# Carrying a written-out instruction order from the up projection into the first six weight groups of a Winograd-form down projection, and moving two kinds of low parts to other units

## The chip, the cores and the metric

The kernel runs on one core of a Trainium2 chip. The metric is the device time of one execution in microseconds (us). Before the change three runs gave 781.72, 781.77 and 783.16 us; the median is 781.77 us.

## The reference, cut to what matters

One decoder layer on 512 tokens of width 1024: an mLSTM and a convolution group with one output projection, then a feed-forward block with a causal convolution of width 3. The change lies wholly in the second half of this feed-forward block:

```python
u = rms_norm(x, ffn_pre_g[l]) * (1.0 + sc2) + sh2
up = causal_dwconv(u @ ffn_up[l], ffn_conv_w[l], ffn_conv_b[l])   # 512 x 5632
a, gt = jnp.split(up, 2, axis=-1)
f = (jax.nn.silu(gt) * a) @ ffn_down[l]                            # 512 x 2816 by 2816 x 1024
x = x + g2 * rms_norm(f, ffn_post_g[l])
```

## The kernel before, in words

Every matrix product is taken in three matmuls (`mm3`, lines 188 to 190): each operand is split into a high part, rounded to the PE's fp32r type, and a low part, the rest. High times high, low times high and high times low are added in PSUM. The high part is a ScalarE copy; the low part is a subtraction, source minus high part. Three helpers make such pairs. `split` (lines 1013 and 1014) subtracts on VectorE. `w_split` (lines 170 and 171) subtracts on GpSimd. `added_split` (lines 1077 to 1079) has ScalarE write the negative of the high part as well and lets a transfer, issued on GpSimd's queue, add the source to it:

```python
S.activation(hi, src, AF.Copy)
S.activation(lo, src, AF.Copy, scale=-1.0)
G.dma_start(lo, src, accum_op=ALU.add)
```

The up projection makes 22 units, numbered 0 to 21, of 128 hidden features; a unit has a value half and a gate half. Units 8, 10, ... 20 are made in a Strassen-Winograd form: seven block products P1 to P7 over halves of the tokens and of the width, four of them opened by `first_products`, then the sums of `between` (lines 1102 to 1107), then the last three. Their odd neighbours are plain. The low part of the form S4, called p3, is made by `added_split`. After its products a unit goes through `conv3` (one ScalarE operation on line 995 and two VectorE operations on line 997 for each half), a silu (line 1132) and the product of value and gate (line 1133), which gives a half of F. Two units make one F, which is `a11, a21, a12, a22` in four quarters. `form_sums` (lines 1021 to 1024) and `form_parts` (lines 1029 to 1033) turn an F into the operands of the down projection: two pairs of high and low tiles (`fh`, `fl`), and two stores, on ScalarE's queue, of what the second stage needs (`g2d`).

The down projection takes the eleven Fs as eleven groups of weights, in the order 4, 5, ... 10, 0, 1, 2, 3 (`ORDER`); the weight groups are numbered by that order, so weight group 6 meets F10, and weight groups 7 to 10 meet F0 to F3, whose operands were written to DRAM and are fetched again by `reload` (line 1318, four transfers each on GpSimd's queue). The first stage makes P1, P5, P7 and P6 for every group, 24 matmuls each. For each group `load1` (lines 1173 and 1177) loads three quarters of 256 KB, `forms1` (lines 1183 to 1185, VectorE) makes three sums of them in place, and `parts1` splits the four forms b1, t1, t3, t2 and stores t2 for later (line 1190). The quarter b1 is not touched by the sums. The second stage makes P2, P3 and P4 with `load2`, `forms2` and `forms_g2`, 18 matmuls a group.

The buffers set much of the order. Weight parts lie in a ring of 20 tiles, two and a half groups. Raw weights lie in four buffers: two of the pool `raws`, which are the ones that held the up projection's raw weights, and two in `more`, which takes the place of `u2h`, the up projection's other operand, and so is free only when the last up-projection matmul has run. `wd_raw` chooses: groups with `m % 4 < 2` go to `raws`, the others to `more`; the first three groups have places of their own. The eight PSUM banks pass from the up projection to the down projection's accumulators: P1 takes two banks, P5 and P7 four, and P6 takes the two banks in which unit 21 lay, so P6 can't start before `conv3` has read unit 21, gate half last (`fg21c`).

What sets the order: PE's matmuls and SyncE's queue go as the code is written. VectorE, ScalarE and GpSimd are ordered by a scheduler, except inside a `with in_order():` block, where what the block holds keeps its written order on each engine. Such a block covers the up projection from unit 8 on and ends with F10's parts. Everything of the down projection after weight group 1 stands outside it:

```python
for m in range(SPILLED):
    reload(m)
for m in range(NM):
    if m > 1:
        forms1(m)
        parts1(m)
    if m + 3 < NM:
        load1(m + 3)
    else:
        load2(m + 3 - NM)
    if m < 5:
        load_g2(m)
    ...
    if m < M1:
        for which in ("p1", "p5", "p7", "p6"):
            prod1(m, which)
```

## Time and profile before

| what | value |
|---|---|
| median of the three runs | 781.77 us |
| the profiled execution: its own time, its span | 782.49 us, 780.8 us |
| PE busy | 757.5 us, 97% of the span |
| VectorE busy | 642.8 us, 82% |
| ScalarE busy | 451.2 us, 58% |
| GpSimd busy | 367.3 us, 47% |
| transfers | 149.00 MB, mean 191 GB/s |

The span runs from the first to the last instruction. The profiled execution's own time is 1.69 us over its span and 0.72 us over the median. Times in rows count from the start of the span. In a timeline the first number is the start, the second the duration, and what stands in square brackets is how long the engine had been idle and what it was waiting for. DVE is VectorE, ACT ScalarE, POOL GpSimd, SP SyncE; an engine's name with a q is its queue.

### The profile page before, as it was taken

To read this page: it belongs to the slowest core of one execution; us is meant where nothing else is said; L and a number is where in the kernel's file an instruction comes from. 1 tells how busy PE (TensorE), PEld (TensorE's weight loads), DVE (VectorE), ACT (ScalarE), POOL (GpSimd) and SP (SyncE) were. 2 spreads that over 40 slices of the span, in tenths; PEclk is the share of its full clock that TensorE was granted. 3 is DMA by queue.
4 is the path that set the end of the run, shared out by engine and by line. 5 is a ranking of instruction groups with operands and counts; after the bars stand their busy time and mean duration, and the time that the engine had idled before them with its cause. 6 is when DMAs were issued, how large, how long until landed. Compare 5 with 4: busy or idle time off the path is not lost.

```text
span 780.8 us, 11567 instructions
## 1 busy us (share of the span) xinstructions
PE 757.5 (97%) x3961; PEld 647.1 (83%) x3961; DVE 642.8 (82%) x1039; ACT 451.2 (58%) x862; POOL 367.3 (47%) x331
## 2 busy tenths in 40 slices
PE   7999999999999999999999999999999998699996
PEld 6888898778888788888889988899988897588885
DVE  6978999999999856837958499788889767898995
ACT  5557275777675266752435466667667674355762
POOL 1039487796796643452831355455455554000001
PEclk9999999999999999999999999999999999799999
DMA  8973225123031551528763598799997989588772
GB/s 330 393 278 121 83 61 186 50 82 108 28 136 54 189 189 55 176 95 288 279 216 135 162 221 238 207 255 240 242 248 185 225 214 317 171 318 253 242 256 107
DMA packets 55263, 149.00 MB, mean 191 GB/s; under 512 B 6402, under 2 KB 7842, under 8 KB 51108
## 3 DMA queue, kind: packets, MB, share of 16 engines
q1 hardware_dynamic: 31284, 96.18, 35.7%
q0 software_dynamic: 9632, 19.40, 12.5%
q10 hardware_dynamic: 14288, 32.68, 12.1%
q8 instruction: 31, 0.51, 0.3%
q14 instruction: 28, 0.23, 0.1%
HBM read 117.42 MB, written 15.61 MB: 170 GB/s over the span
## 4 chain that ended last, share of the span: by engine, by line
PE 58%; DVE 28%; DMA 5%; ACT 4%; issue 3%; POOL 1%; ACTq 0%; SPq 0%; DVEq 0%; POOLq 0%
DVE cv L731 10%; PE up L189 5%; PE up L190 4%; PE up L188 4%; PE p L1415 4%; PE glu L189 3%; PE glu L188 3%; PE glu L190 3%; PE p L189 2%; PE p L188 2%; PE p L190 2%; PE glu L316 2%; PE mixa L190 2%; PE mixa L188 2%; PE mixa L189 2%
## 5 line engine op out<-in xcount | busy, mean ns | idle before, releaser
L731 DVE SCALAR_TENSOR_TENSOR cv<-gt,cvw,cv 128x505 f32<-128x505 f32 (+24 forms) x200 | 137.4, 729 | 2.3 <-ACT cv L719 1.1
L685 POOL TENSOR_TENSOR ro2r<-ro2t,mhalf 128x1 f32<-128x1 f32 x1 | 0.6, 562 | 93.0 <-DVE ro2t L683 93.0
L727 POOL TENSOR_TENSOR cs<-cs,cs 128x510 f32<-128x510 f32 (+3 forms) x32 | 41.7, 1304 | 0.3
L725 ACT ACTIVATE cs<-gt,cvw 128x511 f32<-128x511 f32 (+4 forms) x40 | 27.4, 716 | 5.9 <-POOL cs L727 2.7
L189 PE MATMUL up<-u2l,wup_0h 128*128 128x512 f32 (+1 forms) x72 | 25.7, 356 | 0.2 <-DVE u2l L910 0.2
L188 PE MATMUL up<-u2h,wup_0h 128*128 128x512 f32 (+1 forms) x72 | 25.6, 356 | 0.0
L190 PE MATMUL up<-u2h,wup_0l 128*128 128x512 f32 (+1 forms) x72 | 25.5, 354 | 0.0
L171 POOL TENSOR_TENSOR wglu_0l<-wglu,wglu_0h 128x512 fp32r<-128x512 f32 x4 | 5.3, 1328 | 40.2 <-ACT wglu_0h L170 40.2
L171 POOL TENSOR_TENSOR wqko_1024l<-wqko,wqko_1024h 128x512 fp32r<-128x512 f32 x12 | 15.6, 1297 | 18.4 <-ACT wqko_1024h L170 12.9
L155 DVE SCALAR_TENSOR_TENSOR junk<-spare,cb 128x1024 bf16<-128x1024 f32 x12 | 19.0, 1584 | 3.3 <-DMA spare<-in_adaT 3.1
L155 DVE SCALAR_TENSOR_TENSOR junk<-ada,cb 128x1024 bf16<-128x1024 f32 x12 | 19.5, 1621 | 2.6 <-DMA ada<-in_adaT 2.4
L188 PE MATMUL qko<-uh,wqko_1024h 128*128 128x512 f32 x48 | 20.6, 430 | 0.0
L188 PE MATMUL qko<-uh,wqko_0h 128*128 128x512 f32 x48 | 20.2, 420 | 0.0
L276 DVE SCALAR_TENSOR_TENSOR junk<-ada,cb 128x1024 bf16<-128x1024 f32 x16 | 19.5, 1218 | 0.1
L171 POOL TENSOR_TENSOR wo_512l<-wo,wo_512h 128x512 fp32r<-128x512 f32 x8 | 12.9, 1615 | 13.6 <-ACT wo_512h L170 13.6
L171 POOL TENSOR_TENSOR wqko_0l<-wqko,wqko_0h 128x512 fp32r<-128x512 f32 x12 | 16.6, 1383 | 4.9 <-ACT wqko_0h L170 4.9
L190 PE MATMUL qko<-uh,wqko_1024l 128*128 128x512 f32 x48 | 18.8, 392 | 0.0
L190 PE MATMUL qko<-uh,wqko_0l 128*128 128x512 f32 x48 | 18.8, 391 | 0.0
L171 POOL TENSOR_TENSOR wqko_512l<-wqko,wqko_512h 128x512 fp32r<-128x512 f32 x12 | 17.0, 1420 | 3.7 <-ACT wqko_512h L170 3.7
L189 PE MATMUL qko<-ul,wqko_1024h 128*128 128x512 f32 x48 | 18.7, 390 | 0.0
L189 PE MATMUL qko<-ul,wqko_0h 128*128 128x512 f32 x48 | 18.7, 390 | 0.0
L190 PE MATMUL qko<-uh,wqko_512l 128*128 128x512 f32 x48 | 18.7, 389 | 0.0
(1233 smaller groups left out, 3128.8 us busy)
## 6 DMA issues: line engine op xcount, KB each, us to landing
wups<-in_w_up SPq DMA_DIRECT2D x56, 256.0 KB, 5.5
wqko<-in_w_qko SPq DMA_DIRECT2D x12, 1024.0 KB, 4.8
ada<-in_adaT ACTq DMA_DIRECT2D x20, 512.0 KB, 4.8
ada<-in_adaT SPq DMA_DIRECT2D x16, 512.0 KB, 6.7
wo<-in_w_out SPq DMA_DIRECT2D x8, 1024.0 KB, 4.8
wup<-in_w_up SPq DMA_DIRECT2D x8, 1024.0 KB, 6.2
spare<-in_adaT ACTq DMA_DIRECT2D x12, 512.0 KB, 7.2
wd<-in_w_down SPq DMA_DIRECT2D x20, 256.0 KB, 5.3
```

Of the source, the lines that this page charges most:

```text
L155: t = V.scalar_tensor_tensor(out=junk, in0=r, scalar=1.0, in1=cb, op0=ALU.mult, op1=ALU.mult, accum_out=mod[:, i : i + 1])
L171: (eng or G).tensor_tensor(out=lo[:, :n], in0=src, in1=hi[:, :n].bitcast(F32), op=ALU.subtract)
L188: PE.matmul(ps, a[0], b[0], start=start, stop=False)
L189: PE.matmul(ps, a[0], b[1], start=False, stop=False)
L190: PE.matmul(ps, a[1], b[0], start=False, stop=stop)
L276: V.scalar_tensor_tensor(out=junk, in0=first[k][:, i * D : (i + 1) * D], scalar=1.0, in1=cb, op0=ALU.mult, op1=ALU.mult, accum_out=part[k] ...
L316: PE.matmul(banks0[i], blk(wk, i)[a], u[k][b], start=k == 0 and a == b, stop=False)
L685: G.tensor_tensor(out=r, in0=t, in1=mhalf[:, :1], op=ALU.pow)
L725: S.activation(t[:, d:], cvx[j][:, : T - d], AF.Copy, scale=w(CK - 1 - d))
L727: G.tensor_tensor(out=side[:, d:], in0=side[:, d:], in1=t[:, d:], op=ALU.add)
L731: last_tap[0] = V.scalar_tensor_tensor(out=cp[:, d:], in0=cvx[j][:, : T - d], scalar=w(CK - 1 - d), in1=cp[:, d:], op0=ALU.mult, op1=ALU.add)
L1415: PE.matmul(ps[q], x, y, start=False, stop=m == NM - 1 and i == 2, skip_group_check=True)
```

## The change

What it does, part by part:

- **p3 of the up projection.** The low part of S4 is made by `w_split`, a subtraction on GpSimd, where a second ScalarE copy and an adding transfer made it.
- **b1 of the down projection.** For weight groups 0 to 5 the untouched quarter's low part is made by `added_split`, through the new `part_b`, where VectorE subtracted. Groups 6 to 10 stay as they were.
- **The order.** The block `in_order` now goes on through weight groups 0 to 5, with forms, parts, loads and products written out. `form_parts` is cut in two, `form_highs` and `form_lows`; for F9 the lows are made in weight group 3, and F10's sums and parts come in weight group 4. `between` of unit 20 comes ahead of `forms1(0)`.
- **PE.** P6 of weight group 0 comes after P1 and P5 of weight group 1.
- **Buffers.** `wd_raw` counts `(m - 3) % 4`, so groups 3 and 4 go to `raws` and groups 5 and 6 to `more`.
- **Transfers.** Loads of weight groups 3 and 4 are issued ahead of the last up-projection stores. The sixteen reload transfers, which stood first after the up projection on GpSimd's queue, come one F each in weight groups 5, 6, 7 and 8; the `g2` loads move from groups 0 to 4 to groups 5 to 9.

The core of the diff:

```diff
-    def form_parts(m, F):
+    def form_highs(m, F):
...
+    def form_lows(m, F):
         for (hi, lo), z in zip(pairs[m], (F[:, :T], ysum)):
             V.tensor_tensor(out=lo, in0=z, in1=hi.bitcast(F32), op=ALU.subtract)
...
     def wd_raw(m, n):
-        return raws.tile([P, 2048], F32, tag="raw", name=f"wd{n}_{m}") if m % 4 < 2 else more[:, m % 2, :]
+        return raws.tile([P, 2048], F32, tag="raw", name=f"wd{n}_{m}") if (m - 3) % 4 < 2 else more[:, m % 2, :]
...
+    def part_b(m):
+        w1[m] = {"b1": added_split(loaded[m][1], f"b1_{m}")}
+
+    def parts1(m, a=0, b=3):
+        r = loaded.pop(m) if b == 3 else loaded[m]
+        names = [] if m in w1 else [(f"b1_{m}", 1)]
+        names += [(f"t1_{m}", 2), (f"t3_{m}", 0), (f"t2_{m}", 3)][a:b]
+        w1[m] = w1.get(m, {}) | parts(r, names)
+        if b == 3:
+            nc.sync.dma_start(t2_d[m], r[3])
...
+    def opening_products(m):
+        for which in ("p1", "p5", "p7", "p6"):
+            if m == 1 and which == "p7":
+                prod1(0, "p6")
+            if m or which != "p6":
+                prod1(m, which)
...
-            weight_form(i, "p3", s4, added_split)
+            weight_form(i, "p3", s4)
...
+            between(i, *banks)
             if not more_to_come:
                 forms1(0)
-            between(i, *banks)
...
             else:
+                part_b(0)
+            va = conv3(pa, j, f"fa{j}")
+            if not more_to_come:
                 parts1(0)
                 forms1(1)
-            va = conv3(pa, j, f"fa{j}")
+                part_b(1)
+                for n in (3, 4):
+                    load1(n)
...
-        unit_out(bj, ba, conv3(bg, NF + bj, f"fg{bj}"), Fs[NM - 1])
-        form_sums(NM - 1, Fs[NM - 1])
-        form_parts(NM - 1, Fs[NM - 1])
+        load1(5)
+        bg = conv3(bg, NF + bj, f"fg{bj}")
...
+        opening_products(0)
+        part_b(2)
+        parts1(1, 2)
+        opening_products(1)
+        forms1(2)
+        unit_out(bj, ba, bg, Fs[NM - 1])
+        parts1(2)
+        opening_products(2)
+        for m in range(3, 6):
+            forms1(m)
+            part_b(m)
+            parts1(m)
+            load1(m + 3)
+            if m == 3:
+                form_lows(NM - 2, Fs[NM - 2])
+            elif m == 4:
+                form_sums(NM - 1, Fs[NM - 1])
+                form_parts(NM - 1, Fs[NM - 1])
+            if m > 4:
+                reload(m - 5)
+                load_g2(m - 5)
+            for which in ("p1", "p5", "p7", "p6"):
+                prod1(m, which)
...
-    for m in range(SPILLED):
-        reload(m)
-    for m in range(NM):
-        if m > 1:
-            forms1(m)
-            parts1(m)
+    for m in range(6, NM):
+        forms1(m)
+        parts1(m)
+        if m - 5 < SPILLED:
+            reload(m - 5)
```

**VectorE, around the end of the up projection.** These rows stand on VectorE before, from the product that ends unit 20 on. `fg21c` is the gate half of unit 21, `wdmore` and `wd1_4` are raw weights of groups 3 and 4, `b1_1l` to `t2_1l` are low parts of weight group 1.

```order
L1133 TENSOR_TENSOR F10_6643<-fa20c_6879,fg20c_6883 128x512
L1014 TENSOR_TENSOR b1_1l_6890<-wd1_1_1_6696,b1_1h_6889 128x512
L1014 TENSOR_TENSOR t1_1l_6894<-wd1_1_2_6697,t1_1h_6893 128x512
L1183 TENSOR_TENSOR wdmore_6935<-wdmore_6935 128x512
L1014 TENSOR_TENSOR t3_1l_6898<-wd1_1_0_6695,t3_1h_6897 128x512
L1184 TENSOR_TENSOR wdmore_6935<-wdmore_6935 128x512
L1014 TENSOR_TENSOR t2_1l_6902<-wd1_1_3_6698,t2_1h_6901 128x512
L997 SCALAR_TENSOR_TENSOR fg21c_6906<-up21_1_6854,vec_111,fg21c_6906 128x511
L1014 TENSOR_TENSOR b1_2l_7026<-wd1_2_1_6703,b1_2h_7025 128x512
L1185 TENSOR_TENSOR wdmore_6935<-wdmore_6935 128x512
L1183 TENSOR_TENSOR wd1_4_6995<-wd1_4_6995 128x512
L997 SCALAR_TENSOR_TENSOR fg21c_6906<-up21_1_6854,vec_111,fg21c_6906 128x510
```

And these stand there now:

```order
L1014 TENSOR_TENSOR t1_1l_6890<-wd1_1_2_6692,t1_1h_6889 128x512
L1014 TENSOR_TENSOR t3_1l_6894<-wd1_1_0_6690,t3_1h_6893 128x512
L1139 TENSOR_TENSOR F10_6638<-fa20c_6881,fg20c_6885 128x512
L997 SCALAR_TENSOR_TENSOR fg21c_6902<-up21_1_6856,vec_111,fg21c_6902 128x511
L997 SCALAR_TENSOR_TENSOR fg21c_6902<-up21_1_6856,vec_111,fg21c_6902 128x510
L1014 TENSOR_TENSOR t2_1l_6938<-wd1_1_3_6693,t2_1h_6937 128x512
L1189 TENSOR_TENSOR wd1_2_0_6697<-wd1_2_3_6700,wd1_2_2_6699 128x512
L1190 TENSOR_TENSOR wd1_2_2_6699<-wd1_2_2_6699,wd1_2_1_6698 128x512
```

The two operations of `fg21c` stood behind and between sums on the raw weights of groups 3 and 4; they now follow F10's first half directly, and the next sums are those of group 2.

**ScalarE, at weight group 5.** Before, after unit 21's silu:

```order
L1132 ACTIVATE fg21c_6906<-fg21c_6906 128x512
L1029 ACTIVATE fh10_0_6916<-F10_6643 128x512
L1029 ACTIVATE fh10_1_6918<-ysum_1376 128x512
L1030 DMA g2d10_4537<-F10_6643 128x512
L1031 DMA g2d10_4537<-ysq_1377 128x256
L1013 ACTIVATE g2h0_7321<-g2kept_6936 128x512
```

Now F10's operands come after weight group 4:

```order
L1013 ACTIVATE t2_4h_7078<-wd1_4_6818 128x512
L1029 ACTIVATE fh10_0_7089<-F10_6638 128x512
L1029 ACTIVATE fh10_1_7091<-ysum_1376 128x512
L1030 DMA g2d10_4537<-F10_6638 128x512
L1031 DMA g2d10_4537<-ysq_1377 128x256
L1083 ACTIVATE b1_5h_7126<-wdmore_6899 128x512
L1084 ACTIVATE b1_5l_7127<-wdmore_6899 128x512
```

The store of `ysq` waits for VectorE's last operation of `form_sums`, on which the two copies for b1 of weight group 5 now follow. On VectorE that operation stands right behind the first sum of weight group 7:

```order
L1023 TENSOR_TENSOR ysum_1376<-ysum_1376,F10_6638 128x256
L1189 TENSOR_TENSOR wd1_7_7083<-wd1_7_7083 128x512
L1024 TENSOR_TENSOR ysq_1377<-F10_6638,ysum_1376 128x256
L1035 TENSOR_TENSOR fl10_0_7090<-F10_6638,fh10_0_7089 128x512
L1190 TENSOR_TENSOR wd1_7_7083<-wd1_7_7083 128x512
```

Before, `form_sums` of F10 had its four operations together.

**GpSimd's queue, from the last adding transfer of the up projection on.** Before, the reloads follow at once (the first five of sixteen):

```order
L1079 DMA wup21_3l_6777<-wups1_5084 128x512
L1318 DMA fh0_0b_6937<-own0_4549 128x512
L1318 DMA fl0_0b_6938<-own0_4549 128x512
L1318 DMA fh0_1b_6939<-own0_4549 128x512
L1318 DMA fl0_1b_6940<-own0_4549 128x512
L1318 DMA fh1_0b_6945<-own1_4550 128x512
```

Now six adding transfers stand between:

```order
L1085 DMA wup21_3l_6771<-wups1_5085 128x512
L1085 DMA b1_0l_6787<-wd1_0_6528 128x512
L1085 DMA b1_1l_6812<-wd1_1_1_6691 128x512
L1085 DMA b1_2l_6933<-wd1_2_1_6698 128x512
L1085 DMA b1_3l_7018<-wd1_3_6816 128x512
L1085 DMA b1_4l_7066<-wd1_4_6818 128x512
L1085 DMA b1_5l_7127<-wdmore_6899 128x512
L1212 DMA fh0_0b_7146<-own0_4549 128x512
```

All sixteen reloads have moved behind b1 of weight group 5.

More of the change, by code (lines that the diff above doesn't have):

```diff
@@ L1185, in forms1, with reload, load_g2, part @@
         V.tensor_tensor(out=b22, in0=b22, in1=b12, op=ALU.subtract)
-    def parts1(m):
-        r = loaded.pop(m)
-        w1[m] = parts(r, [(f"b1_{m}", 1), (f"t1_{m}", 2), (f"t3_{m}", 0), (f"t2_{m}", 3)])
-        nc.sync.dma_start(t2_d[m], r[3])
-    w1 = {}
+    def part_b(m):
[7 more added lines that the diff above has]
+            nc.sync.dma_start(t2_d[m], r[3])
+    w1 = {}
+    again = {}
+    def reload(m):
+        again[m] = [(slot(f"fh{m}_{n}b", F32R), slot(f"fl{m}_{n}b", F32R)) for n in range(2)]
+        for n, pair in enumerate(again[m]):
+            for e, z in enumerate(pair):
+                G.dma_start(z.bitcast(F32), own_d[m][:, (2 * n + e) * T : (2 * n + e + 1) * T])
+    M1 = NM - 2
+    M2 = NM - 3
+    fsq = const.tile([P, 2 * NT], F32, name="fsq")
+    def load_g2(m):
+        nc.sync.dma_start(kept[:, m % 5, :], g2_d[ORDER[m]])
+    def part(form, q):
+        return tuple(z[:, q * P : (q + 1) * P] for z in form)
+    def halves_of(pair):
+        return [tuple(z[:, h * HT : (h + 1) * HT] for z in pair) for h in range(2)]
+    def prod1(m, which):
+        (a11, s3), (s1, s2) = (halves_of(z) for z in (pairs[ORDER[m]] if m < NM - SPILLED else again[ORDER[m]]))
+        ps, form, w = {"p1": (p1, a11, "b1"), "p5": (p5, s1, "t1"), "p7": (p7, s3, "t3"), "p6": (p6, s2, "t2")}[which]
+        for q in range(2):
+            mm3(ps[q], part(form, q), w1[m][w], m == 0, m == NM - 1)
+    def opening_products(m):
[4 more added lines that the diff above has]
+                prod1(m, which)
     for m in range(MS):
@@ L1291, in decoder_layer @@
             vx, vz = conv3(X, i, f"fa{i}"), conv3(Z, NF + i, f"fg{i}")
+            if not more_to_come:
+                parts1(1, 0, 2)
             if more_to_come:
@@ L1297, in decoder_layer @@
             unit_out(i, vx, vz, Fs[m])
-            if not more_to_come:
-                parts1(1)
             for n, r in ada[1:]:
@@ L1307, in decoder_layer @@
             before = j, va, pg
+        more = upool.tile([P, 2, 2048], F32, tag="uh", name="wdmore")
+        kept = upool.tile([P, 5, 3 * HT], F32, tag="ul", name="g2kept")
+        load1(5)
         bj, ba, bg = before
-        unit_out(bj, ba, conv3(bg, NF + bj, f"fg{bj}"), Fs[NM - 1])
-        form_sums(NM - 1, Fs[NM - 1])
-        form_parts(NM - 1, Fs[NM - 1])
-    g2r = g2[0]
-    def reload(m):
-        pairs.append([(slot(f"fh{m}_{n}b", F32R), slot(f"fl{m}_{n}b", F32R)) for n in range(2)])
-        for n, pair in enumerate(pairs[-1]):
-            for e, z in enumerate(pair):
-                G.dma_start(z.bitcast(F32), own_d[m][:, (2 * n + e) * T : (2 * n + e + 1) * T])
-    pairs = pairs[SPILLED:]
-    g2_d = [g2_d[m] for m in ORDER]
-    M1 = NM - 2
-    M2 = NM - 3
-    fsq = const.tile([P, 2 * NT], F32, name="fsq")
-    p1 = [atbank(f"p1_{q}") for q in range(2)]
-    p5 = [mmbank(f"p5_{q}") for q in range(2)]
-    p6 = [cvbank(f"p6_{q}") for q in range(2)]
-    p7 = [mmbank(f"p7_{q}") for q in range(2)]
-    more = upool.tile([P, 2, 2048], F32, tag="uh", name="wdmore")
-    kept = upool.tile([P, 5, 3 * HT], F32, tag="ul", name="g2kept")
+        bg = conv3(bg, NF + bj, f"fg{bj}")
+        p1 = [atbank(f"p1_{q}") for q in range(2)]
+        p5 = [mmbank(f"p5_{q}") for q in range(2)]
+        p6 = [cvbank(f"p6_{q}") for q in range(2)]
+        p7 = [mmbank(f"p7_{q}") for q in range(2)]
+        opening_products(0)
[21 more added lines that the diff above has]
+                prod1(m, which)
+    g2r = g2[0]
     def load2(m):
@@ L1354, in forms_g2 @@
         return [(h[:, :HT], l[:, :HT]), (h[:, HT:], l[:, HT:]), (s[:, :HT], s[:, HT:])]
-    def part(form, q):
-        return tuple(z[:, q * P : (q + 1) * P] for z in form)
-    def halves_of(pair):
-        return [tuple(z[:, h * HT : (h + 1) * HT] for z in pair) for h in range(2)]
-    def prod1(m, which):
-        (a11, s3), (s1, s2) = (halves_of(z) for z in pairs[m])
-        ps, form, w = {"p1": (p1, a11, "b1"), "p5": (p5, s1, "t1"), "p7": (p7, s3, "t3"), "p6": (p6, s2, "t2")}[which]
-        for q in range(2):
-            mm3(ps[q], part(form, q), w1[m][w], m == 0, m == NM - 1)
     G2A = 3
     w2, g2 = {}, {}
-    for m in range(SPILLED):
-        reload(m)
-    for m in range(NM):
-        if m > 1:
-            forms1(m)
-            parts1(m)
+    for m in range(6, NM):
[3 more added lines that the diff above has]
+            reload(m - 5)
         if m + 3 < NM:
```

13 lines of the change are left out of this document (8 added, 5 removed).

## The prediction, on record before the run

> **What bounds the kernel now.** I read the page first, then the table of windows over the second half, then PE's waits, then the timelines around the longest one.
>
> ```profile
> PE 757.5 (97%) x3961; PEld 647.1 (83%) x3961; DVE 642.8 (82%) x1039; ACT 451.2 (58%) x862; POOL 367.3 (47%) x331
> core 0: us, PE busy (x) PEld busy (x) DVE busy (x) ACT busy (x) POOL busy (x), PEclk, DMA share, GB/s
> 640.00:660.00 20.00, 19.73 (x107) 16.80 (x106) 17.44 (x31) 11.87 (x22) 8.16 (x13) 1.00 0.95 273
> 660.00:680.00 20.00, 11.67 (x39) 8.94 (x38) 13.10 (x23) 4.54 (x10) 3.30 (x6) 0.74 0.57 205
> 680.00:700.00 20.00, 19.23 (x84) 15.60 (x84) 19.52 (x34) 11.78 (x24) 0.00 (x0) 1.00 0.89 317
> PE p L188 <- DVE fg21c L997: 8.3, 1, 8.3
> PE upx L1086 <- DMA wup_p3l<-s: 1.9, 1, 1.9
> PE p L189 <- DVE t_2l L1014: 0.8, 1, 0.8
> PE upx L1086 <- DVE upx L1106: 0.3, 1, 0.3
> ```
>
> PE is the bound: 97% busy, and its waits in the second half are the four listed. The largest lies in the window 660 to 680, the only one of the three in which the granted clock is under 1. The timeline of PE there:
>
> ```profile
> 656.44 0.39 PE L188 MATMUL p<-b_0h,fh 128*128 128x512 f32 x1
> 660.97 0.39 PE L190 MATMUL p<-t_0h,fl 128*128 128x512 f32 x1
> 669.69 0.77 PE L188 MATMUL p<-t_0h,fh 128*128 128x512 f32 x1 [8.33 <-DVE fg21c L997]
> 675.37 0.47 PE L189 MATMUL p<-t_1l,fh 128*128 128x512 f32 x1
> 675.68 0.39 PE L190 MATMUL p<-t_1h,fl 128*128 128x512 f32 x1
> 679.78 0.39 PE L190 MATMUL p<-b_2h,fl 128*128 128x512 f32 x1
> 681.41 0.50 PE L189 MATMUL p<-t_2l,fh 128*128 128x512 f32 x1 [0.77 <-DVE t_2l L1014]
> 681.75 0.40 PE L190 MATMUL p<-t_2h,fl 128*128 128x512 f32 x1
> ```
>
> The down projection starts at 656.44 and takes 20 steps to 660.97, 0.2265 us each. Then P6 of group 0 waits for its bank. Why `fg21c` was late stands on VectorE and SyncE:
>
> ```profile
> 658.72 0.69 DVE L1014 TENSOR_TENSOR t_1l<-wd,t_1h 128x512 fp32r<-128x512 f32 x1
> 663.39 0.69 DVE L1183 TENSOR_TENSOR wdmore<-wdmore 128x512 f32<-128x512 f32 x1 [3.98 <-DMA wdmore<-in_w_down]
> 668.80 0.74 DVE L997 SCALAR_TENSOR_TENSOR fg21c<-up,vec,fg21c 128x510 f32<-128x510 f32 x1
> 656.63 0.33 SPq L1173 DMA_DIRECT2D wdmore<-in_w_down  x1
> ```
>
> VectorE stood behind a sum on weights whose load was issued only at 656.63, when `u2h` fell free. `fg21c`, PE's releaser, stood behind it.
>
> **What the change gives back.** (a) The wait: 660.97 to 669.69 is 8.72 us for a step of 0.23, so 8.49. (b) The low clock: the 14 matmuls from 669.69 to 675.68 took 5.99 us where 14 x 0.2265 is 3.17, so 2.82. (c) Group 2's late part: 679.78 to 681.75 is 1.97 us for three steps, 0.68, so 1.29. (d) p3, 1.94, and (e) the last sum before unit 20's P2, 0.28.
>
> (a) goes if `fg21c` is done by P6's new place. P6 needs the second bank 33 matmuls into the down projection, at 656.44 + 33 x 0.2265 = 663.9. I retime VectorE from these rows:
>
> ```profile
> 643.09 0.69 DVE L1183 TENSOR_TENSOR wd_0t<-wd_0b,wd 128x512 f32<-128x512 f32 x1
> 645.15 0.42 DVE L1104 TENSOR_TENSOR u<-upx,p 128x256 f32<-128x256 f32 x1
> 646.67 0.68 DVE L1033 TENSOR_TENSOR fl<-F,fh 128x512 fp32r<-128x512 f32 x1
> 652.34 1.53 DVE L997 SCALAR_TENSOR_TENSOR fa21c<-up,vec,fa21c 128x511 f32<-128x511 f32 x2
> 680.67 1.89 DVE L1014 TENSOR_TENSOR t_2l<-wd,t_2h 128x512 fp32r<-128x512 f32 x3
> 645.60 0.63 ACT L1013 ACTIVATE b_0h<-wd 128x512 fp32r<-128x512 f32 x1 [1.21 <-issue]
> 679.46 1.65 ACT L1013 ACTIVATE t_2h<-wd 128x512 fp32r<-128x512 f32 x3
> ```
>
> Three forms take 645.15 - 643.09 = 2.06, `between` 646.67 - 645.15 = 1.52, a convolution half 1.5, a low part 0.6 (three in 1.89), a ScalarE copy 0.55 (three in 1.65), a sum of half width 0.42. From 643.09 `between` and `forms1(0)` end at 646.7. ScalarE still starts b1 of group 0 at 645.60, and behind its two copies the first convolution step, so `fa21c` runs on VectorE from 647.4 to 648.9. Then three lows 1.8, forms 2.06, unit 20's two convolutions 3.0, two lows 1.2, F 0.6, `fg21c` 1.5: 659.1, almost five us early. No load stands ahead of it, since groups 3 and 4 now lie in `raws`, which need not wait for `u2h`. (b) goes with (a). (c) goes too: group 2's parts end at 659.1 + 0.6 + 2.06 + 0.6 + 1.8 = 664.2, PE needs the first of them at 656.44 + 48 x 0.2265 = 667.3. (e) goes since `between` is earlier by 2.06.
>
> (d) The adding transfer was late; now GpSimd subtracts:
>
> ```profile
> 596.73 0.89 POOL L1079 DMA_DIRECT2D wup_p3l<-s  x1 [2.15 <-DVE fg15c L997]
> 605.58 0.38 PE L1086 MATMUL upx<-u2h,wup_p3l 128*128 128x256 f32 x1 [1.94 <-DMA wup_p3l<-s]
> 592.96 1.62 POOL L171 TENSOR_TENSOR wup_p4l<-wups,wup_p4h 128x512 fp32r<-128x512 f32 x1
> 630.76 1.29 POOL L171 TENSOR_TENSOR wup_p5l<-wups,wup_p5h 128x512 fp32r<-128x512 f32 x1
> 630.84 1.75 DVE L1285 TENSOR_TENSOR wups<-wups 128x512 f32<-128x512 f32 x1
> ```
>
> At 596.73 plus at most 1.62 it is there by 598.4, seven us before PE. Of its seven units only this one made PE wait; 1.94 is the most, and it could be 0 if another wait took its place. I take 1.94, since no other wait near it is listed. The last two rows show what speaks against the move: a subtraction on VectorE that began beside GpSimd's took 1.75 where its like takes 0.69. One such clash a unit costs VectorE 1.06; PE waited for VectorE's sums once, 0.28, so the bounds are 0 and 1.06 and I take 0, with VectorE at 82%. The Trainium skill, SBUF — State Buffer, section "Who interferes with whom", has the rule: a VectorE instruction with both inputs in SBUF and a GpSimd one that reads SBUF exclude each other for a whole instruction. The trace agrees with its 1.75; by the rule alone seven clashes would cost VectorE, not PE, 7.4 us.
>
> Sum given back: 8.49 + 2.82 + 1.29 + 1.94 + 0.28 = 14.82.
>
> **What it adds.** The seven dropped p3 copies on ScalarE and six new ones for b1 nearly cancel, and VectorE loses six lows, 3.6 us; ScalarE at 58% covers its part. The adding transfers for b1 and the loads land so:
>
> ```profile
> DMA to landing us min/median/max: 5.1/6.0/6.7
> DMA to landing us min/median/max: 3.3/6.0/9.0
> 643.21 0.41 ACTq L1031 DMA_DIRECT2D g2d<-ysq  x1
> 645.18 0.59 POOL L1318 DMA_DIRECT2D fh_0b<-own  x1 [0.30 <-DMA wup_p3l<-s]
> 671.29 0.55 POOL L1318 DMA_DIRECT2D fl_1b<-own  x1 [4.45 <-PE p L189]
> DMA to landing us min/median/max: 2.8/6.2/8.5
> ```
>
> The first row is `load1`'s transfers of 768 KB, the second all adding transfers of line 1079, the last the reloads. By the same retiming b1 of groups 0 to 4 is sent about 647, 650, 658, 663 and 668 and needed at 656.7, 660.7, 667.5, 673 and 678.4: even 9.0 us just does.
>
> Group 5 is another matter. VectorE goes from 664.2 through group 3's forms and lows (3.86) and F9's lows (1.2) to 669.3, through six forms and three lows of groups 4 and 5 (about 5.6) to 674.9, and through three of F10's sums (1.3) to 676.2. There stands the first sum of group 7. Its load is behind the store of group 4's t2, which is ready four operations after 669.3, at 671.9; it goes at 672.2 and lands 6.0 later, 678.2: VectorE waits 2.0. Behind it `ysq` ends at 678.2 + 0.7 + 0.42 = 679.3; ScalarE's queue holds its store (0.41) and only then the two copies for b1 of group 5 (1.1), so the transfer goes at 680.8 and lands at 684.1 to 689.8, 686.8 at the median. PE needs it at 656.44 + 121 x 0.2265 = 683.8, less the 0.28 of (e): 683.5. A new wait of 0.6 to 6.3; I take the median's 3.3.
>
> The reloads, 16 of 256 KB, move from 645.18 to 671.29 to behind that transfer, about 681. Their cover before was PE's own stall. Group 7 is due at 656.44 + 168 x 0.2265 = 694.5, plus 3.3. I cost them at 0, between 0 and 8.8 (below).
>
> So 14.82 - 3.3 = 11.5; the profiled execution would take 782.49 - 11.5 = 771.0. It is 0.72 above the median; in terms of the median I predict 770.3 us.
>
> **The rivals.** First, the new wait lowers the clock again. 1.94 of idle at 605.58 left the next matmul at 0.38, 8.33 doubled it to 0.77; 3.3 lies between. Then (b)'s 2.82 returns: 773.1. The Trainium skill, TensorE: Matmul & The Clock Gate, section "HAM oscillation — how this bites in real kernels", draws the line at idle gaps over about 3.4 us. By that rule the 6.3 end would pay and the 0.6 end would not; the trace's two gaps agree.
>
> Second, the transfers become the bound from 681 to 707. By the tile sizes the reloads are 4.2 MB, loads and t2 stores of almost five groups 5.0, three g2 loads 1.2: 10.4 MB. At the 317 GB/s of 680 to 700 that takes 32.8 us, at the 273 of 640 to 660, which had reloads in it, 38.1; there are 26 plus the wait of 3.3. PE would be 3.5 to 8.8 later: 773.8 to 779.1, say 775.5. For it: the DMA shares 0.89 and 0.95. Against: two of the loads and two g2 loads aren't due before the second stage.
>
> Third, slower: the reloads alone run so slowly that PE stands before each of groups 7 to 10. The thirteenth, the first of group 10, is due at 656.44 + 222 x 0.2265 + 3.3 = 710.0 and lands 6.2 after issue, so from 681 a pace of 22.8 / 12 = 1.9 us a transfer suffices. They went at 26.11 / 15 = 1.74, with waits for buffers in it. Each 0.1 over 1.9 costs 1.2; from 2.9 the gain is gone, and at 3.2 the time is 770.3 + 15.6 = 785.9.
>
> Fourth, no change: `fg21c` still late, by another load or ScalarE, and (a) to (c) stay: 781.8 less at most (d) and (e), 779.5 to 782.
>
> **How the numbers follow.** Forecast 0.54, its own range 767.0 (no new wait: 782.49 - 14.82 - 0.72) to 773.3 (6.3); clock 0.16; transfers 0.19; slower 0.05; no change 0.06. A range of 766.5 to 777.0 leaves out the upper part of the second rival and the last two, about 0.18. Over 0.2%, 1.56 us, is about what a measurement of this kernel tells from no change. Faster: the first three and a third of the fourth, 0.91; same 0.04; slower 0.05.
>
> **What would show it.** Right: PE's waits list no `fg21c`, P6 of group 0 starts unhindered near 663, the clock in 660 to 680 is 1.00, no wait on `wup_p3l`. The step on group 5 is right if PE's L189 waits on `b_5l` near 683 and VectorE waits for a load of `wd` ahead of `ysq`. Wrong: PE waiting on `fh_0b` or on any b1 of groups 0 to 4, a granted clock under 1 after 690, or a DMA share near 1 with PE waiting from 690 to 710.

## The result and the profile after

| | before | after |
|---|---|---|
| median of the runs | 782.46 us (4 runs, 781.72 to 784.23) | 772.98 us (4 runs, 772.66 to 773.30) |
| ratio, 95% interval | | 0.9876, 0.9857 to 0.9895 |
| profiled execution: its own time, its span | 782.49, 780.8 us | 773.06, 771.3 us |
| first matmul of the up projection | 414.69 | 414.83 |
| first matmul of the down projection | 656.44 | 654.61 |
| last matmul of the down projection | 773.57 | 764.15 |

The change saves 9.5 us by the medians. The forecast was 770.3 in a range of 766.5 to 777.0; the result is 2.7 above the one and inside the other. In the profiled executions the saving is 9.43. Of it 1.83 lies ahead of the down projection, and the down projection itself went from 117.13 to 109.54 us, 7.59 less. It has 11 x 24 + 11 x 18 = 462 matmuls. A step is the time from one matmul's start to the next one's, 0.2265 us where nothing waits, and 461 steps make 104.4. So there are some 5 us of new waits in it, where 12.6 had been before.

PE's waits in the second half, from the list of waits (engine, what it waited for, us in total, times, longest):

```profile
PE p L1462 <- DVE sp L1455: 1.2, 1, 1.2
PE p L188 <- ACT b_10h L1013: 1.0, 1, 1.0
PE upx L1092 <- ACT wup_p1h L170: 0.8, 1, 0.8
PE p L189 <- DMA b_5l<-wdmore: 0.6, 1, 0.6
PE p L189 <- DVE b_10l L1014: 0.2, 1, 0.2
PE p L1462 <- DVE p L1450: 0.2, 1, 0.2
PE up L190 <- DMA wup_0l<-wups: 0.2, 1, 0.2
```

`fg21c`, `wup_p3l` and `t_2l` are gone. In their place stand small waits for the operands of weight groups 5 and 10, and two at the start of the second stage. The windows show where they lie (columns as in the prediction's table; the last three are the granted clock, the DMA share and GB/s):

```profile
660.00:680.00 20.00, 20.00 (x90) 16.57 (x89) 17.98 (x32) 9.07 (x17) 2.32 (x4) 1.00 0.60 171
680.00:700.00 20.00, 19.43 (x86) 15.75 (x85) 13.99 (x24) 9.50 (x18) 9.05 (x17) 1.00 0.95 336
700.00:720.00 20.00, 18.82 (x82) 14.97 (x81) 17.88 (x31) 13.95 (x27) 0.00 (x0) 1.00 0.99 366
720.00:740.00 20.00, 18.55 (x81) 14.71 (x80) 20.00 (x36) 12.54 (x27) 0.00 (x0) 1.00 0.93 321
```

From 660 to 680 PE is busy throughout at the full clock, where it had 11.67 of 20 at 0.74. From 680 to 740 it loses 3.2 us, beside transfers that run at a share of 0.93 to 0.99. VectorE around these places, from its timeline:

```profile
656.05 1.53 DVE L997 SCALAR_TENSOR_TENSOR fg21c<-up,vec,fg21c 128x511 f32<-128x511 f32 x2
670.06 0.69 DVE L1189 TENSOR_TENSOR wdmore<-wdmore 128x512 f32<-128x512 f32 x1 [0.92 <-DMA wdmore<-in_w_down]
676.43 0.69 DVE L1189 TENSOR_TENSOR wd<-wd 128x512 f32<-128x512 f32 x1 [0.94 <-issue]
681.10 0.69 DVE L1191 TENSOR_TENSOR wdmore<-wdmore 128x512 f32<-128x512 f32 x1
682.10 1.89 DVE L1014 TENSOR_TENSOR t_5l<-wdmore,t_5h 128x512 fp32r<-128x512 f32 x3 [0.31 <-PE p L190]
692.22 0.69 DVE L1189 TENSOR_TENSOR wd<-wd 128x512 f32<-128x512 f32 x1 [5.21 <-DMA fh_1b<-own]
```

`fg21c` ends at 657.6, with no wait for a load ahead of it. The second row is the first sum of weight group 6, not of group 5; the third is group 7's. The last sum of group 5 is the fourth row, at 681.10, directly ahead of its low parts. So the scheduler had put the sums of groups 6 and 7, which stand behind the written block, ahead of group 5's, which stand in it. The last row is group 8's first sum, after 5.21 us of idling. The profile names a reload, `fh_1b`, as what ended this wait; the sum itself reads the load that was issued at 682.31, and no row shows when that landed. What hangs on group 5's late sums is on SyncE's queue:

```profile
671.80 0.37 SPq L1179 DMA_DIRECT2D wd<-in_w_down  x1
681.82 0.32 SPq L1202 DMA_DIRECT2D t2d<-wdmore  x1
682.31 0.33 SPq L1179 DMA_DIRECT2D wd<-in_w_down  x1
682.69 0.48 SPq L1220 DMA_DIRECT2D g2kept<-g2d  x1
```

The store of group 5's t2 can go only behind its last sum, at 681.82. The load of group 8 and the first `g2` load stand behind it, so for almost 10 us this queue issues nothing; then it issues all at once, together with the reloads on GpSimd's queue (GpSimd's timeline, first and last of the sixteen, behind b1 of group 5):

```profile
679.42 0.89 POOL L1085 DMA_DIRECT2D b_5l<-wdmore  x1 [11.38 <-DVE fl L1035]
679.98 0.91 POOL L1212 DMA_DIRECT2D fh_0b<-own  x1
696.55 0.55 POOL L1212 DMA_DIRECT2D fl_1b<-own  x1 [0.50 <-issue]
```

The transfers from 680 to 710 (issues: KB each, median us to landing):

```profile
DMA packets 3636, 10.62 MB, mean 354 GB/s; under 512 B 512, under 2 KB 512, under 8 KB 3633
g2kept<-g2d SPq DMA_DIRECT2D x5, 384.0 KB, 8.8
wdmore<-in_w_down SPq DMA_DIRECT2D x2, 768.0 KB, 10.1
fh_0b<-own POOLq DMA_DIRECT2D x4, 256.0 KB, 8.8
```

And before, in the same stretch:

```profile
DMA packets 2712, 8.51 MB, mean 284 GB/s; under 512 B 298, under 2 KB 298, under 8 KB 2709
wd<-in_w_down SPq DMA_DIRECT2D x3, 768.0 KB, 6.1
wdmore<-in_w_down SPq DMA_DIRECT2D x3, 768.0 KB, 5.5
```

The two loads of 768 KB in the list, those of groups 9 and 10, take 10.1 us to land, where loads of this size took 5.5 and 6.1 before. Issued late and landing late, the loads make VectorE's and ScalarE's work on groups 8 to 10 and on the second stage's operands late; PE waits at group 10 and at the start of the second stage.

### The profile page after: what moved, and what is told of

Its sections match the earlier page's. It is cut to its first block, busy times and chain, and to the rows that moved or that the text cites. A ratio compares the mean times of both kernels' runs of the same rounds, so it can differ in the third digit from the quotient of the medians.

```text
span 771.3 us, 11559 instructions
## 1 busy us (share of the span) xinstructions
PE 755.5 (98%) x3961; PEld 644.7 (84%) x3961; DVE 638.5 (83%) x1033; ACT 448.9 (58%) x861; POOL 376.4 (49%) x337
## 4 chain that ended last, share of the span: by engine, by line
PE 48%; DVE 28%; DMA 9%; ACT 6%; issue 4%; POOL 3%; ACTq 1%; SPq 1%; POOLq 0%; DVEq 0%
DVE cv L731 10%; PE p L1462 4%; PE glu L189 3%; PE glu L190 3%; PE glu L188 3%; PE up L190 3%; PE up L189 3%; PE up L188 3%; PE glu L316 2%; PE upx L1092 2%; PE mixa L190 2%; PE mixa L188 2%; PE mixa L189 2%; PE mixb L188 2%; PE mixb L190 2%
## 5 line engine op out<-in xcount | busy, mean ns | idle before, releaser
L171 POOL TENSOR_TENSOR wo_1024l<-wo,wo_1024h 128x512 fp32r<-128x512 f32 x8 | 11.6, 1451 | 14.9 <-ACT wo_1024h L170 14.9
```

The lines of the kernel that those rows point to most:

```text
L171: (eng or G).tensor_tensor(out=lo[:, :n], in0=src, in1=hi[:, :n].bitcast(F32), op=ALU.subtract)
```

## The experiments

The theory on trial: the gain of terms (a) to (c) comes from the place of `fg21c` in VectorE's order; what the change leaves on the table, some 5 us, comes from the late sums of group 5 and from the reloads that are issued in the same burst. The rivals: that VectorE was relieved, that the buffers did it, that PE's deferral of P6 did it, and that the bytes as such are the bound. "Stretch" below is first to last matmul of the down projection in each profiled execution, as above 117.13 before and 109.54 after. It is the steadier measure for the parts behind the up projection: in the profiled executions of the change and of e3 to e12, whose up projection is the same but for b1 of the first groups, the down projection began anywhere from 653.57 to 655.99. It is still one execution for each kernel. Each ratio is to runs of before that belong to that run; their median was 783.86 for e1 to e4, 782.42 for e5 to e8, 782.11 for e9 to e11 and 782.07 for e12. Runs of different sets are therefore better compared by the ratio or the stretch than by the medians.

| run | median, us | ratio to before, 95% interval | stretch, us |
|---|---|---|---|
| after | 772.98 | 0.9876, 0.9857 to 0.9895 | 109.54 |
| e1_p3 | 780.36 | 0.9954, 0.9936 to 0.9971 | 115.74 |
| e2_raw | 784.09 | 1.0010, 0.9992 to 1.0028 | 117.16 |
| e3_b1_vector | 775.75 | 0.9901, 0.9880 to 0.9922 | 112.36 |
| e4_p6_plain | 772.90 | 0.9857, 0.9832 to 0.9882 | 108.93 |
| e5_reload | 775.60 | 0.9906, 0.9878 to 0.9934 | 111.53 |
| e6_order | 770.29 | 0.9845, 0.9815 to 0.9875 | 107.18 |
| e7_both | 770.20 | 0.9839, 0.9811 to 0.9867 | 106.46 |
| e8_noreload | 768.91 | 0.9823, 0.9791 to 0.9856 | 106.23 |
| e9_gate_late | 777.74 | 0.9938, 0.9914 to 0.9962 | 114.95 |
| e10_order9 | 770.96 | 0.9847, 0.9821 to 0.9873 | 105.90 |
| e11_order9_reload | 772.10 | 0.9868, 0.9840 to 0.9896 | 108.90 |
| e12_order9_vec | 771.02 | 0.9858, 0.9834 to 0.9882 | 107.90 |

### e4_p6_plain: the deferral on PE

```diff
         for which in ("p1", "p5", "p7", "p6"):
-            if m == 1 and which == "p7":
-                prod1(0, "p6")
-            if m or which != "p6":
-                prod1(m, which)
+            prod1(m, which)
```

> The changed kernel, with P6 of group 0 back in its plain place, behind P7 of group 0 (no deferral on PE). Theory: fg21c now ends at about 657.5 us and P6's second bank is wanted no sooner than 654.61 + 21 x 0.2265 = 659.4, so the deferral is worth nothing: 772.5 to 773.5 us, ratio within 0.001 of the changed kernel's 0.9876. Rival (the deferral on PE carries part of the gain): PE waits for fg21c by 1 to 4 us, and with over 3 us the clock falls too and 2.8 us come on top: 774 to 780 us.

772.90 us and no wait there. VectorE had `fg21c` ready at 658.6:

```profile
657.10 1.53 DVE L997 SCALAR_TENSOR_TENSOR fg21c<-up,vec,fg21c 128x511 f32<-128x511 f32 x2
```

PE began the down projection at 655.59 in this execution and reached the second bank at 660.35. The deferral gave nothing in these runs; it is a reserve of 12 steps, 2.7 us.

### e2_raw: the buffers alone

```diff
-        return raws.tile([P, 2048], F32, tag="raw", name=f"wd{n}_{m}") if m % 4 < 2 else more[:, m % 2, :]
+        return raws.tile([P, 2048], F32, tag="raw", name=f"wd{n}_{m}") if (m - 3) % 4 < 2 else more[:, m % 2, :]
```

> The kernel before, with one other part alone: raw weights of groups 3 and 4 in the pool raws, so that VectorE's sums on group 3 need not wait for u2h. Theory (what counts is that fg21c stands ahead of the sums on weights in VectorE's order): the sums on group 4 still stand around fg21c, and their load stands behind others on SyncE's queue, so PE still waits for fg21c before P6 of group 0, 3 to 9 us of it, and the time is 776 to 783 us, ratio 0.992 to 1.001. Rival (the buffers are what brought the gain): no wait for fg21c on PE, the granted clock 1.00 from 660 to 680, and 10.5 to 12.6 us less, ratio 0.984 to 0.987.

No change: 1.0010, 0.9992 to 1.0028. VectorE still stood ahead of `fg21c`, now in front of the load into the free buffer:

```profile
665.31 0.69 DVE L1183 TENSOR_TENSOR wd<-wd 128x512 f32<-128x512 f32 x1 [5.89 <-DMA wd<-in_w_down]
```

```profile
655.12 0.33 SPq L1190 DMA_DIRECT2D t2d<-wd  x1
655.55 0.38 SPq L1173 DMA_DIRECT2D wd<-in_w_down  x1
```

The load stands behind a t2 store on SyncE's queue and went at 655.55. The down projection began at 659.12 in this execution, so the load went 3.57 us ahead of it, where that of before went 0.19 behind. But it took 9.6 us to land, where that of before took 6.7, so by the same count VectorE's sum started only 0.8 us sooner. PE waited 9.58 us for `fg21c`, more than the 9 at the upper end of the theory's range, and the median lies above its times. A buffer that falls free earlier brought an earlier issue here, but no earlier `fg21c`, as the sum still stood ahead of it. Why the load landed so late isn't shown; reloads ran beside it in both kernels.

### e1_p3: the low part p3 alone

```diff
-            weight_form(i, "p3", s4, added_split)
+            weight_form(i, "p3", s4)
```

> The kernel before, with one part of the change alone: the low part of S4 (p3) subtracted on GpSimd, no second ScalarE copy and no adding transfer. Theory (each term of the prediction stands by itself): PE's wait of 1.94 us on wup_p3l goes and nothing else moves, so the time falls by 1.6 to 1.9 us, to a ratio of 0.9976 to 0.9980; the wait of 8.3 us for fg21c stays. Rival 1 (another wait takes its place, as the 0.77 on wup_p1h and the 0.16 on wup_0l that the changed kernel shows): under 0.8 us, ratio 0.999 to 1.000. Rival 2 (GpSimd's subtraction beside VectorE's sums costs VectorE about 1.06 us a unit and this reaches fg21c): slower by 0.3 to 1.06 us.

Faster, by more than either expectation: 0.9954, 0.9936 to 0.9971, which is 2.3 to 5.0 us. The profiled execution is only 1.61 shorter than that of before (780.88 against 782.49), but its up projection began 1.07 later (415.76 against 414.69), behind two waits of PE in an earlier stage that the edit doesn't touch: 1.44 and 0.68, where before had 0.27 and none. From the first matmul of the up projection to the first of the down projection it took 240.48 in place of 241.75, 1.27 less. The wait on `wup_p3l` is gone there, but 0.73 on `wup_p1h` has appeared and the wait of (e) has grown from 0.28 to 0.68, so the first rival holds in part. Another 1.39 is in the stretch, by a wait for `fg21c` of 7.54 in place of 8.33 and eleven steps at the low clock in place of fourteen:

```profile
668.70 0.77 PE L188 MATMUL p<-t_0h,fh 128*128 128x512 f32 x1 [7.54 <-DVE fg21c L997]
673.10 0.45 PE L189 MATMUL p<-t_1l,fh 128*128 128x512 f32 x1
```

Together that is 2.66 us, inside the interval. The 1.27 lies where p3 is used; why `fg21c` came earlier in the stretch isn't shown.

### e3_b1_vector: b1 by VectorE again

```diff
     def part_b(m):
-        w1[m] = {"b1": added_split(loaded[m][1], f"b1_{m}")}
+        pass
```

> The changed kernel, with the low part of b1 of groups 0 to 5 subtracted by VectorE again instead of by adding transfers. Theory (the order, not the relieved VectorE, brought the gain): VectorE gets 3.6 us more work, two lows (1.2 us) of it ahead of fg21c, which ends at 657.5 and would end at 658.7; PE needs it at 663 after P6's deferral, so no wait comes back. The wait on b_5l (0.57 us idle, 0.73 of step) goes. Time 772.0 to 774.0 us, ratio 0.9866 to 0.9892. Rival (VectorE's relief counts): its 3.6 us reappear on PE, late parts or fg21c, and the time is 776 to 785 us, ratio 0.992 or more.

775.75 us, between the two expectations. But the cost isn't spread over six groups. It is in one place, PE's timeline at group 5, with VectorE's beside it:

```profile
683.53 0.50 PE L188 MATMUL p<-b_5h,fh 128*128 128x512 f32 x1 [1.08 <-ACT b_5h L1013]
687.43 0.80 PE L189 MATMUL p<-b_5l,fh 128*128 128x512 f32 x1 [3.40 <-DVE b_5l L1014]
692.24 0.39 PE L188 MATMUL p<-t_5h,fh 128*128 128x512 f32 x1
```

```profile
673.79 0.69 DVE L1189 TENSOR_TENSOR wdmore<-wdmore 128x512 f32<-128x512 f32 x1 [3.42 <-DMA wdmore<-in_w_down]
686.69 0.68 DVE L1014 TENSOR_TENSOR b_5l<-wdmore,b_5h 128x512 fp32r<-128x512 f32 x1
```

VectorE waits 3.42 us for group 6's load and does the sums of groups 6 and 7 before it comes to group 5's low part. The clock falls as well: eleven steps from 687.43 to 692.24 took 4.81 in place of 2.49. So it is the sums from behind the written block that cost here. That the six subtractions by themselves don't is shown only by e12, below.

### e9_gate_late: is it the place of fg21c?

This is the direct test. In e4's kernel, the nine sums of weight groups 2 to 4 go ahead of the gate half; nothing is added.

```diff
         load1(5)
+        for m in (2, 3, 4):
+            forms1(m)
         bj, ba, bg = before
         bg = conv3(bg, NF + bj, f"fg{bj}")
...
-        forms1(2)
...
         for m in range(3, 6):
-            forms1(m)
+            if m > 4:
+                forms1(m)
```

> The kernel of e4_p6_plain (the changed kernel with P6 of group 0 in its plain place), with VectorE's nine sums on weight groups 2, 3 and 4 ahead of the gate half of unit 21, about where the scheduler had such sums before. VectorE's work stays the same. Theory (the place of fg21c on VectorE is what brought the gain of terms (a) to (c)): in e4 fg21c ended at 658.6 and P6's second bank was wanted at 660.35; nine sums of 0.69 take 6.2, so fg21c ends at 664.8, PE waits 3.8 to 5 us, and the clock falls behind it as in e3_b1_vector (3.4 us of wait, some 2 us): 776 to 780 us against e4's 772.9. Rival (VectorE's relieved load, not its order, brought the gain): PE's wait stays under 1 us and the time at 772.5 to 774 us.

777.74 us against e4's 772.90. By the ratios e9 is 0.0081 above e4, some 6.3 us, and the stretch is 6.0 longer. VectorE and PE:

```profile
661.68 1.53 DVE L997 SCALAR_TENSOR_TENSOR fg21c<-up,vec,fg21c 128x511 f32<-128x511 f32 x2
```

```profile
663.35 0.76 PE L188 MATMUL p<-t_0h,fh 128*128 128x512 f32 x1 [4.31 <-DVE fg21c L997]
663.91 0.63 PE L189 MATMUL p<-t_0l,fh 128*128 128x512 f32 x1
667.01 0.40 PE L188 MATMUL p<-t_1h,fh 128*128 128x512 f32 x1
```

The wait of before is back, 4.31 us of it, and with it the low clock: the nine steps from 663.35 to 667.01, the last of them at the normal pace again, took 3.66 where 9 x 0.2265 is 2.04. That is 6.1 us in this place; behind it, longer waits and a second fall of the clock at group 10 and the waits that are missing at group 5 and in the second stage about cancel. Work and transfers were those of e4. So terms (a) and (b) are shown: they hang on what stands ahead of `fg21c` on VectorE. What wasn't run is the new order with the old buffers, so it isn't shown that the order alone, with group 3's load still waiting for `u2h`, would bring the gain.

### e6_order, e7_both, e5_reload: the late sums, the burst of reloads

e6 carries the block on through groups 6 and 7; e5 issues the reloads two groups earlier; e7 does both.

```diff
-        for m in range(3, 6):
+        for m in range(3, 8):
             forms1(m)
-            part_b(m)
+            if m < 6:
+                part_b(m)
...
-    for m in range(6, NM):
+    for m in range(8, NM):
```

```diff
-            if m > 4:
-                reload(m - 5)
-                load_g2(m - 5)
+            reload(m - 3)
+            if m > 4:
+                load_g2(m - 5)
...
-        if m - 5 < SPILLED:
-            reload(m - 5)
+        if m - 3 < SPILLED:
+            reload(m - 3)
```

> The changed kernel, with the sixteen reload transfers issued two weight groups earlier (in groups 3 to 6 instead of 5 to 8), into the stretch 660 to 680 where the DMA share is 0.60. Theory (what is left to gain, 4.9 us, comes from a jam of transfers from 681 to 710: share 0.95 to 0.99, loads landing in 9 to 10 us instead of 5 to 6): the waits on b_10h and b_10l (1.6 us) go and some of the 1.8 us in the second stage, less up to 1 us more on b_5l, whose transfer now has eight reloads ahead of it: 770.5 to 772.5 us, ratio 0.984 to 0.987. Rival (the late stores and loads on SyncE's queue, behind group 5's sums, are enough by themselves): 772.5 to 774 us, ratio 0.987 to 0.989.

> The changed kernel, with the written-out order carried on through weight groups 6 and 7, so that VectorE makes the sums of group 5 ahead of those of groups 6 and 7; reloads stay where they are. Theory (group 5's sums behind those of groups 6 and 7 delay its t2 store to 681.8, and behind that on SyncE's queue the load of group 8 and the g2 loads, into the burst of reloads): the store goes some 5 to 8 us earlier, the wait on b_5l (0.7) goes and those on b_10h and b_10l shrink: 770.5 to 772.3 us, ratio 0.984 to 0.987. Rival (the bytes bound the stretch whatever their order): 772.5 to 773.5 us, and the waits only move. Other way out: the scheduler's own order was as good, and the fixed order makes PE wait at groups 6 or 7: over 774 us.

> The changed kernel with both: the written-out order through weight groups 6 and 7, and the reloads two groups earlier. Theory (both spread the transfers of 681 to 710): 769 to 771 us, ratio 0.982 to 0.985, less than either alone. Rival (one of the two is enough or they cost elsewhere): no less than the better of the two by 0.3 us.

e6: 770.29 us, stretch 107.18; e7: 770.20, 106.46; e5: 775.60, 111.53, worse than both of its expectations and, though its interval overlaps the change's, worse than the change by all three columns. e6 is a little under its theory's range. In e6 group 5's store goes six us earlier, five if counted from the start of the down projection, and group 8's load with it:

```profile
675.74 0.32 SPq L1202 DMA_DIRECT2D t2d<-wdmore  x1
676.23 0.73 SPq L1179 DMA_DIRECT2D wd<-in_w_down  x1
```

In e5 the reloads ran beside group 6's load, which landed in 8.3 us where the loads of that stretch took 4.9 in the change. VectorE stood 4.26 us before it, ahead of group 5's sums; the store came still later, at 685.64, and PE waited 2.1 us for `b_5l` and 0.9 for `b_10l`. The burst did get smaller: 9.04 MB from 680 to 710 in place of 10.62, and the two loads in the list landed in 6.5 us in place of 10.1. The waits at group 10 and in the second stage shrank with it, from 3.7 us of PE's time to 2.0. But 2.6 were lost at group 5 in place of 0.8, and 1.1 at group 7, where nothing had been. So earlier reloads alone only move the loss to an earlier place, as long as the sums of groups 6 and 7 stand ahead of group 5's. (A further 0.9 of e5's stretch is a wait on `b_0l` at its start, ahead of anything that the edit moves.) With the order right, the reloads' place is worth nothing that can be told (e6 against e7). The half of the theory about the order holds. The half about the reloads doesn't hold by itself; e7's time lies in its theory's range, but it is only 0.09 under e6's, so the rival's expectation is the one that holds.

### e8_noreload: no reloads at all

```diff
     def reload(m):
-        again[m] = [(slot(f"fh{m}_{n}b", F32R), slot(f"fl{m}_{n}b", F32R)) for n in range(2)]
-        for n, pair in enumerate(again[m]):
-            for e, z in enumerate(pair):
-                G.dma_start(z.bitcast(F32), own_d[m][:, (2 * n + e) * T : (2 * n + e + 1) * T])
+        again[m] = pairs[m + 7]
```

> The changed kernel without the sixteen reload transfers: weight groups 7 to 10 are multiplied with the operands of F7 to F10 again, so 4.2 MB are not fetched and the first stage's last four groups compute something else. Theory (the jam of transfers bounds 681 to 740): the waits on b_10h, b_10l and in the second stage go, 3.4 us: 769 to 770.3 us, ratio 0.982 to 0.984, DMA share from 680 to 720 under 0.8. Rival (the order of VectorE and of SyncE's queue, not the bytes): under 1 us less, 772 to 773 us, the waits on b_10 and in the second stage stay.

This kernel leaves out the fetches of 4.2 MB and multiplies the last four groups with the operands of others. 768.91 us, stretch 106.23, and PE full from 700 to 720:

```profile
700.00:720.00 20.00, 20.00 (x89) 16.33 (x88) 19.01 (x34) 13.40 (x26) 0.00 (x0) 1.00 0.89 304
```

Without the reloads the waits at group 10 and at the start of the second stage go too, although group 5's store still goes at 680.93. The time is just under the theory's range; the DMA share isn't as the theory had it: 0.93 and 0.89 in the windows 680 to 700 and 700 to 720, not under 0.8. So the late sums and the reloads make the loss together: taking away either one takes most of it, and e6 does it without leaving any work out.

### e10_order9, e11_order9_reload, e12_order9_vec: the written order carried on further

In e6 VectorE stood 5.75 us at group 8's first sum, again a sum from behind the block, ahead of low parts of group 6:

```profile
686.93 0.69 DVE L1189 TENSOR_TENSOR wd<-wd 128x512 f32<-128x512 f32 x1 [5.75 <-DMA wd<-in_w_down]
687.54 1.29 DVE L1014 TENSOR_TENSOR t_6l<-wdmore,t_6h 128x512 fp32r<-128x512 f32 x2
```

e10 writes group 8 out too (`range(3, 9)`, with `load2` and `forms_g2` in the loop). e11 has the reloads one group earlier as well, `reload(m - 4)`. e12 is e10 with `part_b` left empty as in e3.

> The changed kernel, with the written-out order carried on through weight groups 6, 7 and 8, reloads as in the change. In e6_order the first sum of group 8, outside the order, stood ahead of two low parts of group 6 and the forms of group 7, and VectorE waited 5.75 us there for group 8's load; PE's wait of 1.4 on b_7l followed. Theory (what stands outside the written order still goes ahead and brings waits for loads): that wait on PE goes: 768.5 to 769.8 us, ratio 0.982 to 0.9835. Rival (the bytes bound the stretch, the wait only moves to group 8 or 9): 769.8 to 771 us.

> The same as e10_order9, with the reloads one weight group earlier (groups 4 to 7), so that four reloads instead of eight (e7_both) or none (e10_order9) stand ahead of b1 of group 5 on GpSimd's queue. Theory (bytes spread into 660 to 680 help once the order is written, at some price on b_5l, which waited 1.7 in e7_both): 768 to 769.5 us, ratio 0.981 to 0.983. Rival (with the order written, the place of the reloads doesn't matter, as e6_order and e7_both hint): within 0.5 us of e10_order9.

> The kernel of e10_order9, with the low part of b1 of weight groups 0 to 5 subtracted by VectorE, as before the change, instead of by adding transfers. Theory (in e3_b1_vector it was the sums of groups 6 and 7 ahead of group 5's low part that cost 3.4 us of wait and the clock, not the six subtractions themselves): with the order written, the six lows (3.6 us) stay beside PE's work; group 5's low part ends at about 680 and is wanted at about 682: no wait on b_5l, 770 to 772 us, within 1 us of e10_order9's 770.96, ratio 0.983 to 0.987. Rival (VectorE needs the relief): PE waits for low parts by 1 to 4 us in all, 772 to 776 us.

e10's stretch is the shortest, 105.90 of a possible 104.4, with one wait of 0.55 in it. The window that had been the bound:

```profile
680.00:700.00 20.00, 20.00 (x90) 16.57 (x89) 14.84 (x25) 9.39 (x19) 5.55 (x11) 1.00 1.02 376
```

PE is full beside a DMA share of 1.02, higher than the 0.95 of the change. From 680 to 710 11.32 MB are moved, 0.7 more than in the change, and loads of 768 KB take the same 10.1 us to land; but the loads of groups 9 and 10 are issued at 681.48 and 690.52, six us earlier than the 687.69 and 696.12 of the change. The wait on `b_7l` went, as expected, but the median, 770.96, is not lower than e6's 770.29: the stretch gained 1.3, and the runs' scatter (769.32 to 771.37) is larger. By the time the rival's range holds; by its sign, a wait that moves to group 8 or 9, it doesn't.

e11 is 772.10, 1.1 above e10, and has one long wait. On VectorE the low parts of `g2` for three groups and all three sums of group 10 stood ahead of group 10's first low part; in e10 it was two groups' `g2` and one sum:

```profile
704.16 0.39 PE L188 MATMUL p<-b_10h,fh_0b 128*128 128x512 f32 x1
707.06 0.73 PE L189 MATMUL p<-b_10l,fh_0b 128*128 128x512 f32 x1 [2.50 <-DVE b_10l L1014]
710.57 0.40 PE L188 MATMUL p<-t_9h,fh_1b 128*128 128x512 f32 x1
```

Neither its theory nor its rival holds.

e12 is 771.02 against e10's 770.96. VectorE makes `b_5l` at 680.52, in time, and PE waits for no b1. The stretch is 2.0 longer than e10's by waits for VectorE in the second stage (1.3 and 0.8), the medians are the same. So the adding transfers for b1 are worth nothing that these runs can tell, once the order keeps groups 6 and 7 behind group 5; in the change itself, where it doesn't, they were worth 2.8 by the stretch and 2.0 by the ratios (e3, whose interval overlaps the change's).

Of the versions that leave nothing out, e6, e7, e10 and e12 are 1.4 to 2.9 us under the change by the ratios, and have stretches 1.6 to 3.6 shorter; but even e7's interval, 0.9811 to 0.9867, overlaps the change's at its end, and the four can't be told from one another.

## Why the prediction was right, and where not

**(a), (b), (c), 12.60: right.** `fg21c` ended 2.97 us after the start of the down projection (657.58 less 654.61); the retiming had 2.66 (659.1 less 656.44). PE doesn't wait for it, the clock stays at 1.00, `t_2l` is in time. e9 puts the cause back and gets the wait and the clock back. That (b) is 2.82 was one execution's draw: the low clock lasted 14 steps before, 11 in e1, 8 in e2 and e9. (c) was not put back by any run; its wait is gone from the list.

**(d) and (e), 2.22: mis-sized by 0.25.** From the first matmul of the up projection to the first of the down projection the trace of before has 241.75 us and that of after 239.78, 1.97 less; that the down projection starts only 1.83 earlier is due to the earlier stages, which were 0.14 slower. The wait on `wup_p3l` is gone and `between` waits no more, but 0.77 on `wup_p1h` and 0.16 on `wup_0l` came up behind them. The prediction took the whole of (d), "since no other wait near it is listed"; a wait that lies behind another isn't listed until the first is gone. VectorE's clashes with GpSimd cost PE nothing that shows, as taken: sums of 1.74 to 1.77 us on `wups` stand six times from 510 to 640 in the trace of after, and six times in that of before.

**The new wait on b1 of group 5: in its bounds, but not at its centre.** It was put at 0.6 to 6.3, and 3.3 taken. The transfer went at 679.42, 24.8 us after the start where the retiming had 24.4, and landed 3.4 later, near the lower end of 3.3 to 9.0. PE lost 0.73. The median was the wrong row (and 6.0 is that of the transfers that read `wups`; over all of line 1079 it is 6.2). In the time of this transfer, 679.42 to 682.82, the DMA share was 0.54, and those of groups 3 and 4 had landed in 3.3 and 4.1; that the share is the reason isn't shown. Where eight reloads stood ahead of it (e5, e7) PE waited 2.1 and 1.7.

**The reloads at 0: wrong, and here the rest of the gain went.** PE lost 1.6 us before group 10 and 1.8 at the start of the second stage, and e8, without reloads, has a stretch 3.3 us shorter. The second rival had named place and signs, a DMA share near 1 and PE waiting from 690 to 710, at 3.5 to 8.8 us. Its size was nearly right, its reason was not: that the bytes as such bound the stretch. e6 moves 10.89 MB from 680 to 710 and e10 11.32, both more than the change's 10.62, with PE waiting less or not at all.

**The step that failed** is in the same paragraph as the new wait: "through six forms and three lows of groups 4 and 5". Those were the sums of groups 4 and 6. The two groups 5 and 6 lie in one tile, `wdmore`, and read alike in the order. With the sums taken for group 5's, its t2 store would go at about 675, and nothing in the prediction looked late; it went at 681.82, and behind it on SyncE's queue went the load of group 8 and the `g2` loads, into the reloads. VectorE did idle ahead of `ysq`, as forecast: 0.94 at group 7's first sum against the 2.0 taken (this profile names no releaser; at the same sum e3's and e5's name the load, 0.99 and 1.57), and 0.92 at group 6's, which had not been seen.

**Sum.** Forecast 14.82 less 3.3, 11.5 in the profiled execution; measured 12.60 + 1.83 less 5.0, 9.43. The sign and the large terms were right; the two cost terms, 3.3 and 0, came to 0.8 and, with all the rest, 4.2. That these two errors went opposite ways is luck: it left the total only 2.1 off in the profiled execution, where the one term was 2.5 too high and the other 4.2 too low.

**The first rival** (the clock falls again at `b_5l`) did not come, as the wait was short. At the 3.3 that the prediction took it likely would have: in e3 3.40 lowered the clock, in e11 2.50 did. The forecast's own value and its neglect of the clock didn't fit together. The third and fourth rival had nothing for them: the reloads' pace was 16.57 / 15 = 1.10 us a transfer.
